# Transposing the attention's softmax weights: one 16-bit transposing transfer in place of four TensorE transposes

## The chip, the cores and the metric

The kernel runs on one core of one Trainium2 chip. A core has five engines, each with its own instruction queue that is worked through in order: TensorE (PE, matrix products; its weight loads are listed as PEld), VectorE (DVE), ScalarE (ACT), GpSimd (POOL) and SyncE (SP), which here only issues transfers. Sixteen DMA engines move the data. Operands lie in SBUF (128 partitions); TensorE writes to PSUM, which is used here as eight banks of 128 x 512 float32. The engines wait for each other through semaphores.

The metric is the time of one execution on the device in microseconds (us), the median of several runs. The profile is of one further execution.

## What is computed

One decoder block on 256 positions of width 2048, all in float32: a normalisation, one wide input projection, two branches (attention and a gated linear recurrence), gates, an output projection, and a gated feed-forward network (FFN). The change touches only the attention:

```python
ATTN_GROUPS = ((128, 1), (512, 4), (2048, 16))      # (window, dilation)
...
for g, (window, dilation) in enumerate(ATTN_GROUPS):
    o_g, lse_g = dilated_window_attention(qh[g], kh[g], vh[g], window, dilation)
    outs.append(o_g)
    lses.append(lse_g)
mix_w = jax.nn.softmax(jnp.stack(lses, axis=0), axis=0)
attn = jnp.einsum('gbhs,gbhsd->bshd', mix_w, jnp.stack(outs, axis=0))
```

There are eight heads with three groups each. A query sees the keys of its group at the group's stride, each group has its own softmax, and the three outputs are mixed by their softmax denominators. This is the same as one softmax over the keys of all three groups together (a key of two groups counted twice), and that is how the kernel computes it.

## The kernel before

**The stream of weights.** Nearly all of the time is matrix products of the activations with weights that are read once. Each float32 product is made of three faster ones: weights and activations are split into a high half (a rounded copy, made by ScalarE) and a low half (the difference, made by VectorE). The main loop runs over "items". In the stage of interest, an item is a chunk of 128 x 1024 weights. For item i the loop emits, in this order: `prepare(i)`, which splits the chunk of item i + 2 (line 365 on ScalarE, line 366 on VectorE, `AHEAD = 2`) and has SP issue loads (`load_pair`, line 270; a pair of chunks fills one of three buffers called raw); `multiply(i)` (line 139, all products); one step of the oldest waiting evacuation of a finished block (lines 240 and 242 add up two banks of accumulation, 888 to 893 apply the rotary tables, 1151 makes gates); `advance_lanes()`, one step of each of two lanes of side work; and `ahead_of_time()`, one step of sums of FFN weights made in advance (`weight_sums`: loads by SP at line 302, sums by VectorE at lines 310 to 314, a store by ScalarE's queue at 317). All instructions stay in this order on each engine (`manual_schedule`), so what is emitted earlier stands ahead in each engine's queue. A split weight chunk has one of three buffers (w), so the split for item i + 2 has to wait until the products of item i - 1 are done.

**The lanes.** They are Python generators: what stands between two `yield`s is emitted in one step, once per item. The recurrence runs in lane 0, twice (half 0, half 1). The attention is taken by lane 1, and by lane 0 too when that is free. It works through a queue of (half, head), four heads for each half of the heads.

**One pass of the attention** is one head and one parity: the 128 queries of even or of odd position. Its 512 scores per query are four blocks of 128 keys: two for the first group (keys of both parities), one for each of the others (keys of the query's parity). A pass takes six steps:

1. TensorE makes the scores in a PSUM bank.
2. VectorE adds the mask and finds the smallest score, whose sign is turned (line 928, into p), and ScalarE takes the exponential with its sum (line 932).
3. VectorE takes the reciprocal of the sum (line 937) and scales p by it (line 938).
4. TensorE transposes the four 128 x 128 blocks of p into a PSUM bank (line 944, against the identity matrix).
5. ScalarE copies the bank to pt in SBUF (line 947), 128 x 512 float32. One more step with nothing follows.
6. TensorE multiplies V with pt, four products that add up to the head's output (in the profile, aux<-pt,v). In the same step the next pass's scores follow.

When a head's two parities are done, `attended` copies its output into the high and low halves for the next projection (lines 966 and 969). p and pt are float32 tiles of 128 x 512 from one ring of five buffers (`ptile`, which also serves the evacuations' short-lived tiles). PSUM banks for the side work (`aux()`) come from a ring of four.

In the first half's passes the items are chunks of the key and query projections; lane 1 works one pass after another beside the recurrence of lane 0, and later both lanes do attention, three steps apart. In the second half's passes (items of the gates and of the recurrence's projection, 12 products of 512 columns each) both lanes are at the same step, so that passes go in pairs.

**Transposing transfers elsewhere.** The FFN turns its activations with `turn_act` (line 1366 on): ScalarE writes the 16-bit halves of each float32 word into two planes (line 1370), SP issues transposing transfers of 128 x 512 two-byte elements (line 1376), and ScalarE joins the transposed planes to words again (line 1385). Its instructions are in the profile of before.

Of the kernel before, what the change touches and what calls it, by code (L numbers as in the profile page):

```python
# [17 lines left out]
U16 = mybir.dt.uint16  # L18
AF = mybir.ActivationFunctionType
OP = mybir.AluOpType  # L20

P = 128
# [79 lines left out]
def tile_hybrid_block(ctx: ExitStack, tc: tile.TileContext, t, out):  # L102
    nc = tc.nc
# [12 lines left out]
    def nm(s):  # L116
        serial[0] += 1
        return f"{s}_{serial[0]}"
# [7 lines left out]
    def aux():  # L126
        return auxp.tile([P, 512], F32, tag="aux", name=nm("aux"))
# [7 lines left out]
    def small(s, n=8, bufs=6):  # L135
        return cpool.tile([P, n], F32, tag=f"small{n}", bufs=bufs, name=nm(s))

    def mm(ps, lhsT, rhs, start, stop):
        nc.tensor.matmul(ps, lhsT, rhs, start=start, stop=stop, skip_group_check=True)  # L139
# [27 lines left out]
    ident = cpool.tile([P, P], F32, name="ident")  # L167
# [38 lines left out]
    def ptile(s):  # L206
        pool, n = (wide_pool[-1], 2) if wide_pool else (fp[0], 5)
        return pool.tile([P, 512], F32, tag="p", bufs=n, name=nm(s))
# [341 lines left out]
            yield  # L550


    class Split:


# [110 lines left out]
    def advance_lanes():  # L666
        tick[0] += 1
        for lane in lanes:
            if not lane and queue:
                lane.append(attention())  # L670
            advance(lane)
# [233 lines left out]
    def attention():  # L905
        done = []
        for _ in range(3):
            if not lanes[0] or tick[0] == beat[0]:
                break
            yield  # L910
        while queue:
            half, h = queue.popleft()
            o = None
            for par in range(2):
                own = slice(par * P, (par + 1) * P)
                ps = aux()
                for g in range(3):
                    q, k = qkT["q", half, g], qkT["k", half, g]
                    if g == 0:
                        mm(ps[:, :S], q[:, h, own], k[:, h, :], True, True)  # L920
                    else:
                        mm(ps[:, P * (g + 1) : P * (g + 2)], q[:, h, own], k[:, h, own], True, True)
                yield
                for part in done[:1]:
                    part()
                p = ptile("p")
                m = small("m")
                nc.vector.tensor_tensor_reduce(
                    out=p, in0=ps, in1=amask[:, par, :], scale=1.0, scalar=3e38,
                    op0=OP.add, op1=OP.min, accum_out=m[:, 0:1],  # L930
                )
                nc.scalar.activation(p, p, AF.Exp, scale=-1.0, bias=m[:, 0:1], accum_out=m[:, 1:2])
                for part in done[1:]:
                    part()
                done = []
                yield
                nc.vector.reciprocal(m[:, 2:3], m[:, 1:2])
                nc.vector.tensor_scalar(p, p, m[:, 2:3], None, op0=OP.mult)
                for _ in range(1):
                    yield  # L940
                ps = aux()
                for c in range(4):
                    cols = slice(c * P, (c + 1) * P)
                    nc.tensor.transpose(ps[:, cols], p[:, cols], ident)  # L944
                yield
                pt = ptile("pt")
                nc.scalar.activation(pt, ps, AF.Copy)
                for _ in range(2):
                    yield
                if o is None:  # L950
                    o = aux()
                for c in range(4):
                    v = vN[half, max(c - 1, 0)][:, c if c < 2 else par, h * P : (h + 1) * P]
                    mm(o[:, own], v, pt[:, c * P : (c + 1) * P], c == 0, c == 3)
            done = attended(4 * half + h, o)
        yield
        for part in done:
            part()
        yield

    def attended(k, o):
        hi, lo, _ = attnT[0](k)
        ov = o[:, :S].rearrange("p (two j) -> p two j", two=2)

        def high():
            nc.scalar.activation(hi.rearrange("p (j two) -> p two j", two=2), ov, AF.Copy)

        def low():
            nc.vector.tensor_sub(
                lo.rearrange("p (j two) -> p two j", two=2), ov,  # L970
                attnT[0].f32(k).rearrange("p (j two) -> p two j", two=2),
            )

        return [high, low]
# [602 lines left out]
    for half in range(2):  # L1577
        for g in range(3):
            c = 1024 * g + 512 * half
# [54 lines left out]
    for i in range(len(items)):  # L1634
        kind, n, _ = items[i]
        b, c = kind[n][:2]
# [99 lines left out]
```

## Time and profile before

| | |
|---|---|
| median of 3 runs | 1688.17 us |
| lowest and highest run | 1687.39 and 1688.42 us |
| the profiled execution | 1689.89 us |
| its span, first to last instruction | 1688.1 us |
| granted TensorE clock, mean | 0.999 of full speed |
| the attention's transposes (line 944) | 64, between 613.9 and 842.1 us |

A row of an instruction group reads: line, engine, operation, output<-inputs by the program's names, shapes, count, then its duration (mean, or smallest/median/largest in ns) and what ended the engine's idle time before it. A row of the timeline begins with the start and the length in us. A row of the chain of waits has the start, the length and the engine that the end of the program can be traced back to. SPq, ACTq and so on are an engine's instruction sequencer: it waits, or issues transfers, while the engine itself does nothing.

### The profile page before, as it was taken

To read this page: it belongs to the slowest core of one execution; us is meant where nothing else is said; L and a number is where in the kernel's file an instruction comes from. 1 tells how busy PE (TensorE), PEld (TensorE's weight loads), DVE (VectorE), ACT (ScalarE), POOL (GpSimd) and SP (SyncE) were. 2 spreads that over 40 slices of the span, in tenths; PEclk is the share of its full clock that TensorE was granted. 3 is DMA by queue.
4 is the path that set the end of the run, shared out by engine and by line. 5 is a ranking of instruction groups with operands and counts; after the bars stand their busy time and mean duration, and the time that the engine had idled before them with its cause. 6 is when DMAs were issued, how large, how long until landed. Compare 5 with 4: busy or idle time off the path is not lost.

```text
span 1688.1 us, 21672 instructions
## 1 busy us (share of the span) xinstructions
PE 1674.2 (99%) x8169; PEld 1406.0 (83%) x8169; DVE 1416.6 (84%) x1623; ACT 983.1 (58%) x1102; POOL 3.9 (0%) x13
## 2 busy tenths in 40 slices
PE   9999999999999999999999999999999999999997
PEld 7888888888888888888888888888888888888886
DVE  6899888867987987776668888898888988898987
ACT  6655555544455545555535547676667666675653
POOL 0000000000000000000000000000000000000000
PEclk9999999999999999999999999999999999999999
DMA  8566666668777866787858556898888888887673
GB/s 278 207 232 242 224 226 227 234 231 298 233 251 250 281 226 225 254 307 264 309 175 274 194 183 209 272 282 270 272 266 283 271 274 266 277 280 267 236 256 128
DMA packets 252841, 419.26 MB, mean 248 GB/s; under 512 B 36752, under 2 KB 103488, under 8 KB 250176
## 3 DMA queue, kind: packets, MB, share of 16 engines
q1 hardware_dynamic: 242480, 379.70, 68.1%
q10 hardware_dynamic: 10192, 38.15, 5.9%
q8 instruction: 64, 1.05, 0.3%
q14 instruction: 41, 0.34, 0.1%
q0 software_dynamic: 64, 0.02, 0.0%
HBM read 376.92 MB, written 35.13 MB: 244 GB/s over the span
## 4 chain that ended last, share of the span: by engine, by line
PE 95%; DVE 2%; ACT 1%; DMA 1%; issue 1%; SPq 0%; DVEq 0%; ACTq 0%
PE acc L139 62%; PE aux L139 32%; DVE wl L421 1%; PE aux L944 0%; DMA raw<-in_w_ffn_gate_up 0%; ACT w L419 0%; DMA x<-in_x 0%; PE aux L611 0%; DVE fz L1509 0%; DVE dl L431 0%; ACT junk L1463 0%; PE aux L598 0%; DVE e L1459 0%; DVE wl L428 0%; DVE f L543 0%
## 5 line engine op out<-in xcount | busy, mean ns | idle before, releaser
L139 PE MATMUL acc<-xT,w 128*128 128x256 f32 (+1 forms) x2048 | 365.1, 338 | 0.0
L421 DVE TENSOR_TENSOR wl<-raw,w 128x2048 fp32r<-128x2048 f32 (+1 forms) x140 | 304.5, 2182 | 67.3 <-ACT w L419 65.3
L139 PEld LDWEIGHTS acc<-xT,w 128*128 128x128 f32 x2048 | 311.9, 188 | 44.7
L366 DVE TENSOR_TENSOR w<-raw,w 128x1024 fp32r<-128x1024 f32 x176 | 215.0, 1222 | 118.9 <-ACT w L365 118.3
L419 ACT ACTIVATE w<-raw 128x2048 fp32r<-128x2048 f32 (+1 forms) x140 | 254.5, 1826 | 97.4 <-PE acc L139 31.6
L365 ACT ACTIVATE w<-raw 128x1024 fp32r<-128x1024 f32 x176 | 185.9, 1058 | 192.8 <-PE acc L139 137.4
L139 PE MATMUL acc<-w,xT 128*128 128x512 f32 x578 | 168.8, 391 | 0.0
L440 ACT ACTIVATE w<-sum 128x1024 fp32r<-128x1024 f32 x57 | 60.6, 1062 | 168.5 <-DVE sum L435 161.7
L139 PE MATMUL acc<-w,hT 128*128 128x512 f32 x472 | 152.7, 391 | 0.4 <-DVE hT L1259 0.4
L448 DVE TENSOR_TENSOR wl<-sum,w 128x1024 fp32r<-128x1024 f32 x114 | 137.2, 1221 | 7.7 <-ACT w L440 7.6
L139 PEld LDWEIGHTS acc<-w,xT 128*128 128x128 f32 x578 | 108.2, 188 | 22.3
L139 PE MATMUL aux<-w,hT 128*128 128x512 f32 x374 | 120.0, 389 | 0.0
L139 PE MATMUL aux<-w,xT 128*128 128x512 f32 x344 | 109.8, 389 | 0.0
L450 DVE TENSOR_TENSOR dl<-raw,dh 128x1536 fp32r<-128x1536 f32 x57 | 100.1, 1757 | 11.3 <-ACT dh L446 8.2
L139 PEld LDWEIGHTS acc<-w,hT 128*128 128x128 f32 x472 | 88.5, 188 | 19.0 <-DVE hT L1259 0.9
L139 PE MATMUL acc<-wl,hT 128*128 128x512 f32 x236 | 91.8, 389 | 0.0
L446 ACT ACTIVATE dh<-raw 128x1536 fp32r<-128x1536 f32 x57 | 84.1, 1475 | 5.3 <-PE acc L139 3.1
L139 PE MATMUL acc<-w,a 128*128 128x512 f32 x268 | 83.7, 389 | 0.2 <-DVE e L1413 0.2
L139 PEld LDWEIGHTS aux<-w,hT 128*128 128x128 f32 x374 | 70.2, 188 | 14.5
L139 PE MATMUL acc<-w,so 128*128 128x512 f32 x240 | 80.4, 389 | 0.0
L139 PE MATMUL aux<-w,a 128*128 128x512 f32 x254 | 79.5, 389 | 0.0
L139 PEld LDWEIGHTS aux<-w,xT 128*128 128x128 f32 x344 | 64.6, 188 | 13.4
(295 smaller groups left out, 2990.2 us busy)
## 6 DMA issues: line engine op xcount, KB each, us to landing
raw<-in_w_in SPq DMA_DIRECT2D x270, 512.0 KB, 4.7
raw<-in_w_ffn_gate_up SPq DMA_DIRECT2D x156, 512.0 KB, 5.0
raw<-in_w_ffn_down SPq DMA_DIRECT2D x88, 512.0 KB, 5.4
pre<-in_w_ffn_gate_up SPq DMA_DIRECT2D x40, 512.0 KB, 6.5
presum<-pre ACTq DMA_DIRECT2D x20, 1024.0 KB, 4.7
s<-presum SPq DMA_DIRECT2D x40, 512.0 KB, 6.9
raw<-in_w_mix_out SPq DMA_DIRECT2D x32, 512.0 KB, 5.0
act<-acts SPq DMA_DIRECT2D x22, 512.0 KB, 6.2
```

What stands on the lines that cost most here:

```text
L139: nc.tensor.matmul(ps, lhsT, rhs, start=start, stop=stop, skip_group_check=True)
L365: nc.scalar.activation(wh, raw, AF.Copy)
L366: nc.vector.tensor_sub(wl, raw, wh.bitcast(F32))
L419: nc.scalar.activation(hi[:, c], raw[:, c], AF.Copy)
L421: nc.vector.tensor_sub(lo[:, c], raw[:, c], hi[:, c].bitcast(F32))
L440: nc.scalar.activation(hi[:, :1024], s[:, :1024], AF.Copy)
L446: nc.scalar.activation(dhi, d, AF.Copy)
L448: nc.vector.tensor_sub(lo[:, c], s[:, c], hi[:, c].bitcast(F32))
L450: nc.vector.tensor_sub(dlo, d, dhi.bitcast(F32))
```

## The change

The four TensorE transposes of a pass, their PSUM bank and ScalarE's copy out of it go. In their place ScalarE splits the 32-bit words of the normalised p into two planes of 16-bit halves (into the tile pt, used as scratch), one transfer issued by SP transposes all eight 128 x 128 blocks of 16-bit elements back into p, and ScalarE joins the two transposed planes of p to words in pt. The bits are moved unchanged. The copy apart and the transfer are emitted in the step of the normalisation (step 3 above), the join three steps later, one step ahead of the products with V. A pass has as many steps as before.

```diff
+    def halves_apart(flat, words):
+
+        nc.scalar.activation(
+            flat.bitcast(U16).rearrange("p (z c) -> p z c", z=2),
+            words.bitcast(U16).rearrange("p (c z) -> p z c", z=2), AF.Copy,
+        )
+
+    def halves_joined(words, planes):
+
+        nc.scalar.activation(
+            words.bitcast(U16).rearrange("p (c z) -> p z c", z=2), planes, AF.Copy
+        )
+
...
                 nc.vector.reciprocal(m[:, 2:3], m[:, 1:2])
                 nc.vector.tensor_scalar(p, p, m[:, 2:3], None, op0=OP.mult)
-                for _ in range(1):
+                pt = ptile("pt")
+                halves_apart(pt, p)
+                nc.sync.dma_start_transpose(
+                    p.bitcast(U16).rearrange("p (n q) -> p n q", n=8), pt.bitcast(U16)
+                )
+                for _ in range(3):
                     yield
-                ps = aux()
-                for c in range(4):
-                    cols = slice(c * P, (c + 1) * P)
-                    nc.tensor.transpose(ps[:, cols], p[:, cols], ident)
+                halves_joined(pt, p.bitcast(U16).rearrange("p (z c) -> p z c", z=2))
                 yield
-                pt = ptile("pt")
-                nc.scalar.activation(pt, ps, AF.Copy)
-                for _ in range(2):
-                    yield
                 if o is None:
                     o = aux()
```

## The prediction

> **What bounds the kernel now.** I read the page first, for which engine is full; then the chain of waits, cut to the stage in which the attention runs; then the rows of the removed instructions.
>
> ```profile
> PE 1674.2 (99%) x8169; PEld 1406.0 (83%) x8169; DVE 1416.6 (84%) x1623; ACT 983.1 (58%) x1102; POOL 3.9 (0%) x13
> PE 95%; DVE 2%; ACT 1%; DMA 1%; issue 1%; SPq 0%; DVEq 0%; ACTq 0%
> by line: PE acc L139 82.4%; PE aux L139 14.4%; PE aux L944 2.9%; PE aux L1137 0.4%; issue 0.1%
> L944 PE MATMUL aux<-ident,p x64: 270/273/328, 614.0 to 842.1; 128*128 128x128 f32 x64
> 600.00:740.00 140.00, 139.85 (x889) 124.54 (x888) 109.86 (x177) 76.90 (x132) 0.00 (x0) 1.00 0.72 246
> 740.00:852.00 112.00, 112.00 (x575) 95.32 (x574) 74.23 (x107) 59.24 (x78) 0.00 (x0) 1.00 0.80 282
> 852.00:1688.00 836.00, 825.60 (x3668) 681.39 (x3666) 730.29 (x760) 518.32 (x506) 0.00 (x0) 1.00 0.76 248
> ```
>
> The first line says that TensorE is busy for 99% of the span; the second that it makes up 95% of the chain that ended last. The third is the chain's share by line for 600 to 850 us alone: nothing but TensorE, with the removed transposes (L944) at 2.9%. The last three give, for each stretch: length, PE, PEld, DVE, ACT, POOL, clock, DMA share, GB/s. PE stands still for 0.15 us in the attention's 252 us, at full clock, with DMA at 0.72 and 0.80. So an instruction removed from PE here is worth its whole place in PE's row, as long as nothing new makes PE wait.
>
> **What the change removes.** 64 transposes (16 passes: 8 heads, 2 parities, 4 each). The mean duration of 273 ns is no price, since matmuls overlap. Their place in the chain is 2.9% of 250 us = 7.2 us; from the pieces of the chain:
>
> ```profile
> 614.14 0.44 PE aux L944 x4
> 779.03 0.87 PE aux L944 x8
> ```
>
> 0.44 us for one pass, 0.87 for two passes side by side, so 16 x 0.44 = **7.0 us**. I take 7.0. Also removed: ScalarE's copy of the transposed bank, 0.59 us per pass, and one PSUM bank per pass. Nothing on PE waits for a bank in this stage (its idle time above), so I give the bank nothing.
>
> **What it adds on ScalarE.** The same pair of copies and the same kind of transfer already run in the FFN:
>
> ```profile
> L1370 ACT ACTIVATE e<-e x20: 1037/1042/1060, 1089.7 to 1468.8; 128x1024 uint16<-128x1024 uint16 x20
> L1385 ACT ACTIVATE act<-e x20: 1337/1374/1385, 1101.5 to 1482.2; 128x1024 uint16<-128x1024 uint16 x20
> L947 ACT ACTIVATE pt<-aux x16: 576/588/612, 614.6 to 843.1; 128x512 f32<-128x512 f32 x16
> ```
>
> Planes apart cost 1.04 us, joined 1.37, less the old 0.59: 1.82 us more per pass, 29 us in all, on an engine with 136 of 252 us busy. That is hidden if the weight splits queued behind it (L365, then VectorE's L366) still beat PE. The worse part is a new wait: the copy apart stands in ScalarE's queue ahead of the next split, and it waits for VectorE's normalisation L938. The tightest place I found is the first pair of passes in the second half:
>
> ```profile
> 776.39 1.06 ACT L365 ACTIVATE w<-raw 128x1024 fp32r<-128x1024 f32 x1 [1.66 <-PE acc L139]
> 777.47 1.28 ACT L1151 ACT_TABLE_LOAD   x1
> 778.76 0.69 ACT L1151 ACTIVATE gate<-acc,r1c 128x512 f32<-128x512 f32 x1
> 776.09 0.49 DVE L938 TENSOR_SCALAR p<-p,m 128x512 f32<-128x512 f32 x1
> 776.69 0.49 DVE L938 TENSOR_SCALAR p<-p,m 128x512 f32<-128x512 f32 x1
> 777.48 1.23 DVE L366 TENSOR_TENSOR w<-raw,w 128x1024 fp32r<-128x1024 f32 x1 [0.31 <-ACT w L365]
> 779.66 8.45 PE L139 MATMUL acc<-w,xT 128*128 128x512 f32 x36
> 787.95 1.05 PE L139 MATMUL aux<-pt,v 128*128 128x128 f32 x8
> ```
>
> Both normalisations end at 777.2. ScalarE then does: apart 776.6 to 777.7, apart 777.7 to 778.7, the split of 776.39 only now, 778.7 to 779.8; VectorE's low half follows, to 781.1. PE's 36 matmuls are three weight chunks of 2.82 us; this split feeds the second, which began at 779.66 + 2.82 = 782.5 and begins 0.87 earlier without the transposes, at 781.6. Half a microsecond is left. The next: table load, gate, split to 782.8, low half to 784.1, wanted at 784.4: 0.3 us. So ScalarE fits, barely. Of the eight single passes of the first half, the tightest I found is the fourth:
>
> ```profile
> 676.13 0.49 DVE L938 TENSOR_SCALAR p<-p,m 128x512 f32<-128x512 f32 x1
> 677.86 1.22 DVE L366 TENSOR_TENSOR w<-raw,w 128x1024 fp32r<-128x1024 f32 x1
> 681.04 5.82 PE L139 MATMUL acc<-xT,w 128*128 128x512 f32 x32
> 686.70 1.05 PE L139 MATMUL aux<-pt,v 128*128 128x128 f32 x8
> ```
>
> Apart 676.6 to 677.7, split to 678.8, its low half 678.8 to 680.0 in place of 677.86 to 679.1, wanted by the chunk at 681.04, now 680.6: 0.6 us left. I allow a stall of 0.25 us for each of the four pairs, **1.0 us** in all; the bounds are 0 and, if every one of 12 steps (8 single, 4 pairs) lost 0.5 us, 6.0. In the same bounds goes that pt is claimed two steps earlier from a ring of five buffers: with two passes under way, seven are claimed in six steps, one comes round after 4.3, and pt is held for 4. That fits, so I cost it at nothing.
>
> **What it adds on SP and DMA.** One transfer per pass of 128x1024 two-byte elements, on SP's queue, behind the weight loads (L270) and ahead of the loads for the weight sums (L302). Its kind:
>
> ```profile
> L1376 SPq DMA_TRANSPOSE e<-e x40: 1217/1610/2399, 1093.5 to 1476.8; - x40
> DMA to landing us min/median/max: 2.5/6.0/8.3
> SPq L270 <- DVE w L366: 138.0, 29, 8.1
> SPq L270 <- DVE m L937: 56.2, 9, 8.5
> 776.01 0.88 SPq L270 DMA_DIRECT2D raw<-in_w_in  x2
> 781.68 7.66 SPq L270 DMA_DIRECT2D raw<-in_w_hgrn_branch  x4
> raw<-in_w_in SPq DMA_DIRECT2D x270, 512.0 KB, 4.7
> ```
>
> Those 40 are 128x512, half the size, so I double the issue: 3.2 us on SP (bounds 1.2, were it fixed, and 4.8). From issue to landing they took 2.5 to 8.3 us, in a stage where four are issued in a row behind loads; twice the data is given 1.6 us of issue and 0.5 of moving more: 4.6 at best, 8.1 in the middle, 10.4 at worst.
>
> The time allowed: from the end of a normalisation to the first product with V is 787.95 - 776.6 = 11.4 us in the pair; the shortest is the fourth pass, 676.6 to 686.7, 10.1 us. Less 1.04, 1.37 and the 0.44 saved, 7.2 us are left for the transfer. SP mostly sleeps in its wait for a free weight buffer (L270); if that wait stands ahead of the transfer, up to 8 us are lost. But the waits ended by L937 show where the transfer falls: the load is released by the split just before the reciprocal (776.01 against L938 at 776.09), and the next load is issued 5.7 us later, at 781.68. The transfer is issued into that hole, and its packets run behind one pair of weight loads only. I take 5.5 us, nearer the best case than the FFN's middle, because here nothing else is queued ahead: inside 7.2. In a pair the second transfer is issued some 3 us after the first, and its product is 1.8 us later, against a window of 11.4, not 10.1: it also fits, with about 1 us.
>
> What is queued behind: the L302 loads come 2 to 6 us later. They feed L310 on VectorE, which can then be held up by 1 to 2 us in the few passes in which both fall together; this is in the 1.0 us above. The weight loads come up to 3 us later, but a buffer is filled six chunks (17 us) before its use and lands in 4.7.
>
> The Trainium skill ("Advanced Engine Details and Errata", X-Bar Transpose) calls such transposes as fast as plain DMAs; by it the transfer's share of the DMA engines is about 1 us per pass, an estimate, and no term changes.
>
> **The sum.** 7.0 removed, 1.0 given back: 6.0 us. The profiled execution took 1689.9 us with a span of 1688.1, and goes to 1683.9 and 1682.1; the median of the runs is 1688.2, so I predict **1682.2**. The measurement cannot tell less than about 0.2% (3.4 us) from no change: faster begins at 1684.8.
>
> **Rivals.**
> - Late splits. The copies apart and the joins hold up ScalarE and VectorE more than I allow, 0.3 to 0.5 us of room being overrun in all 12 steps: 6.0 us given back, 1687.2; with only the pairs overrun by 1 us each, 1685.2. For it: the sums above, and L938 ends where VectorE is 78% busy. Against: the work saved on ScalarE by the old copy.
> - Late transfer, **the slower side**. The join waits for the landing, PE for the join. It decides from 7.2 us on; each step that is late by x costs x. With the FFN's middle, 8.1, 12 steps lose 0.9: 10.8 less 7.0, 3.8 slower, 1692.0. For it: that median, and the issue time that was never seen for this size. Against: the hole in SP's queue, and the FFN's transfers standing four in a row.
> - Blocks one after another. If the whole issue-to-landing time doubles with the size, 12.0 us at the median, each step loses 4.8: 57.6 less 7.0, 1738.8. The Trainium skill ("VectorE: DVE Perf Modes", The three transpose paths) speaks that way: 1309 ns by DMA for one 128x128 block against 390 on TensorE, whose use it advises; eight in a row would be over 10 us. The best landing above speaks against it: four blocks in 2.5 us.
> - Saved but given back. After 852 us PE is idle for 10.4 us in 836; if a later stage runs at DMA's or VectorE's pace, the 7 us turn into idle time there: 1688. PE's 99% there speaks against.
>
> **How the numbers follow.** Forecast (1680.5 to 1684.7) 0.67; late splits 0.15; given back 0.04; late transfer 0.11; blocks in a row 0.03. So faster 0.67, same 0.19, slower 0.14. The range runs from all 7.0 saved, with half a microsecond of scatter, 1680.5, to the end of the cases without loss, 1688.0; outside are the slower cases and a little below.
>
> **What would show it.** Right: L944 is gone; in 600 to 850 us the chain is still all TensorE, PE's idle time stays near 1 us, and the attention's last product comes some 6 us earlier. The new transposes land within 7 us of their issue, and the join's line shows little idle time released by DMA. Wrong: PE waits for pt or for w in that stretch (late transfer, late splits), or the stretch is shorter and PE's idle time after 852 us grows by as much (given back). I would be most wrong if the issue on SP took far longer than 3 us.

## The result, and the profile after

The changed kernel takes **1706.97 us**, the median of 4 runs (1703.08 to 1708.23), beside 1687.88 us for the kernel before (4 runs, 1687.39 to 1688.42): a ratio of 1.0107, with a 95% interval of 1.0095 to 1.0120. It is 1.1% slower, where 6 us less had been forecast. The profiled execution took 1707.22 us, with a span of 1705.4 us and a mean granted clock of 0.992.

In kernel.py of after the two copies of ScalarE stand at lines 555 (planes apart) and 562 (planes joined), the transfer at 954; the lines of the attention that were there before stand 13 lower (the smallest score 941, exponential 945, reciprocal 950, normalisation 951, rotary tables 901 to 906). The lines up to 552, so 139, 242, 270, 302, 310 to 317, 365 and 366, have not moved.

First the page of after (busy time by engine, and the chain of waits), then the chain between 600 and 850 us by line.

```profile
PE 1677.9 (98%) x8105; PEld 1407.4 (83%) x8105; DVE 1416.2 (83%) x1623; ACT 1007.2 (59%) x1118; POOL 3.8 (0%) x13
PE 92%; DVE 3%; ACT 2%; DMA 2%; issue 1%; ACTq 0%; DVEq 0%
```

```profile
by line: PE acc L139 46.2%; PE aux L139 11.9%; DMA p<-pt 11.4%; DVE w L366 7.1%; issue 6.0%; ACT w L365 4.4%; ACT pt L562 2.2%; DVE w L905 1.2%; DVE sum L904 1.2%; DVE p L941 1.2%; DVE sum L242 1.1%; DVE p L951 1.0%; ACT w L901 0.8%; DVE qk
```

PE has 64 instructions fewer, as meant, and is busy for longer (1677.9 us, before 1674.2). Between 600 and 850 us the chain was all TensorE before; now TensorE is 58.1% of it, the transfer p<-pt 11.4%, the copy that joins (L562) 2.2%, and the splits and the work ahead of them (L365, L366, L904, L905, L941, L951) most of the rest.

Where in the span? I cut both traces at the same places of the program: the first half's stretch runs from the first product of the 84th of the 128 chunks of the key and query projections to the last product of the 128th, the second half's on to the first product of the attention's own projection, and that projection up to the output projection. The windows of before, then of after (length, then busy time of PE, PEld, DVE, ACT, POOL, granted clock, DMA share, GB/s):

```profile
598.63:752.73 154.10, 153.95 (x970) 136.86 (x969) 122.00 (x193) 84.01 (x141) 0.00 (x0) 1.00 0.73 251
752.73:857.71 104.98, 104.98 (x529) 88.98 (x529) 66.33 (x95) 54.67 (x72) 0.00 (x0) 1.00 0.78 270
```

```profile
597.21:767.99 170.78, 158.42 (x938) 139.67 (x937) 122.31 (x193) 96.02 (x149) 0.00 (x0) 0.95 0.79 239
767.99:875.92 107.93, 104.14 (x497) 87.02 (x496) 65.51 (x95) 66.76 (x80) 0.00 (x0) 0.98 0.91 282
875.92:922.20 46.28, 46.28 (x218) 38.29 (x216) 35.67 (x47) 22.17 (x23) 0.00 (x0) 1.00 0.57 185
```

Length less PE's busy time is PE's idle time: in the first half 0.15 us before and 12.36 after, in the second 0 and 3.79. The second loss is the clock: a mean of 0.95 of full speed over 170.78 us is 8.5 us lost (from the clock's own records: 8.53, and 1.71 in the second half; 1.3 of the 8.5 fall on time in which PE stands anyway). Take that off, and PE's work at full clock fell from 153.95 to 151.2 us and from 104.98 to 102.4: 2.8 and 2.5, so **5.3 us of the 7.0 did go**. Against that stand 16.0 us of new idle time and 8.9 of half clock: 19.6 us more in the two stretches. The rest of the span is 2.3 us shorter; 1.4 of that lies before 597 us, where the change has no part.

What PE waited for, by the view of the waits, in after between 600 and 870 us (in all, times, the longest; before, this list is empty):

```profile
PE aux L139 <- ACT pt L562: 13.9, 5, 4.2
PE acc L139 <- DVE w L366: 1.5, 2, 0.8
PE acc L139 <- ACT w L365: 0.7, 1, 0.7
```

So 13.9 us are five waits of the products with V for the joined pt, and only 2.2 us are waits for split weights. What such a wait does to the clock is seen in three neighbouring windows around the longest of the five:

```profile
685.00:689.90 4.90, 0.69 (x4) 0.32 (x3) 1.29 (x2) 1.39 (x2) 0.00 (x0) 0.87 1.02 300
689.90:695.30 5.40, 5.40 (x20) 4.93 (x21) 3.98 (x7) 3.41 (x7) 0.00 (x0) 0.50 1.05 362
695.30:712.00 16.70, 16.70 (x98) 14.53 (x96) 10.88 (x17) 7.73 (x12) 0.00 (x0) 1.00 0.64 145
```

PE stands for 4.2 us, then works at a granted clock of 0.50 for 5.4 us. By the clock records the four waits of 4.21, 3.14, 3.60 and 2.34 us were followed by half clock for 6.8, 3.4, 6.8 and 3.4 us, and the fifth, of 0.65 us, by none. The Trainium skill ("TensorE: Matmul & The Clock Gate", Why this matters for your kernels) asks for no idle gaps of TensorE over about 3 us, since one window of idle halves the clock; this trace agrees, except that 2.34 us were enough.

**Four ways in which pt came late.** The first is seen in the chain of waits of after that ends in the longest stall:

```profile
677.36 11.06 DMA p<-pt
...
688.51 1.35 ACT pt L562
...
689.90 2.50 PE aux L139 x9
```

The transfer is issued as soon as the planes are apart, but lands only 11.06 us later. In that time ScalarE's queue has the store of the FFN's weight sums (L317). The view of the DMA from 677 to 689 us, before and then after (packets, MB, share of the engines' time; below, the median us to landing):

```profile
q10 hardware_dynamic: 144, 1.05, 20.7%
presum<-pre ACTq DMA_DIRECT2D x1, 1024.0 KB, 5.7
```

```profile
DMA  5999999999999000000066946025999949969999
q10 hardware_dynamic: 144, 1.05, 53.1%
presum<-pre ACTq DMA_DIRECT2D x1, 1024.0 KB, 10.3
p<-pt SPq DMA_TRANSPOSE x1, 11.1
```

The store's same 1.05 MB took 20.7% of the engines' time beside plain loads and 53.1% beside the transfer, and landed after 10.3 us and not 5.7; in between, the engines stood nearly still (the zeros, some 2 us).

The second way has nothing to do with the landing. The timeline of after (start, length):

```profile
701.41 1.23 SPq L954 DMA_TRANSPOSE p<-pt  x1
712.43 0.49 DVE L951 TENSOR_SCALAR p<-p,m 128x512 f32<-128x512 f32 x1
712.95 1.06 ACT L555 ACTIVATE pt<-p 128x1024 uint16<-128x1024 uint16 x1 [2.01 <-DVE p L951]
713.91 1.32 ACT L562 ACTIVATE pt<-p 128x1024 uint16<-128x1024 uint16 x1
715.29 1.56 PE L139 MATMUL aux<-pt,v 128*128 128x128 f32 x8 [3.14 <-ACT pt L562]
```

This transfer landed at 707.78, but its join begins at 713.91. The two lanes are three steps apart, so this lane's join is emitted in the very step in which the other lane's planes are taken apart, behind it in ScalarE's queue; and that copy waits for VectorE's normalisation, which ends at 712.92. The next but one pass did the same: joined 7.58 us after its landing, with a stall of 3.60.

The third way is SP's queue:

```profile
708.01 10.33 SPq L270 DMA_DIRECT2D raw<-in_w_in  x4
718.43 1.26 SPq L954 DMA_TRANSPOSE p<-pt  x1
```

The transfer of the planes that were taken apart from 712.95 to 714.00 is issued at 718.43: SP slept in a wait of L270 for a free weight buffer. This befell the sixth and the eighth of the eight passes of the first half (4.4 us each).

The fourth way is loads issued just ahead, among them those of the weight sums (L302). It befell the first pass and the second pair of the second half, whose two transfers are merged in the second row:

```profile
813.00 0.93 SPq L302 DMA_DIRECT2D pre<-in_w_ffn_gate_up  x2
813.99 8.03 SPq L954 DMA_TRANSPOSE p<-pt  x2
```

The first transfer of that pair landed 9.2 us after its issue began, that of the first pass 9.3 us, with no store under way.

What each way cost is seen from the five waits for pt: 4.21 us in the fourth pass (the landing beside the store), 3.14 and 3.60 in the fifth and the seventh (the join's place in ScalarE's queue), 2.34 in the second pair of the second half and 0.65 in the first pass (the loads ahead). The third way cost nothing here: in the sixth and the eighth pass no product waited. It comes to bear in the experiments.

The transfer itself, by its line (smallest, median and largest duration of the issue in ns; then us to landing):

```profile
L954 SPq DMA_TRANSPOSE p<-pt x16: 1232/1882/4047, 612.3 to 862.3; - x16
DMA to landing us min/median/max: 5.0/6.3/11.1
```

Counted from the end of the copy apart, the eight passes of the first half landed after 9.7, 5.4, 8.1, 11.1, 6.4, 9.7, 5.0 and 10.0 us.

### The profile page after: what moved, and what is told of

Its sections match the earlier page's. It is cut to its first block, busy times and chain, and to the rows that moved or that the text cites. A ratio compares the mean times of both kernels' runs of the same rounds, so it can differ in the third digit from the quotient of the medians.

```text
span 1705.4 us, 21609 instructions
## 1 busy us (share of the span) xinstructions
PE 1677.9 (98%) x8105; PEld 1407.4 (83%) x8105; DVE 1416.2 (83%) x1623; ACT 1007.2 (59%) x1118; POOL 3.8 (0%) x13
## 4 chain that ended last, share of the span: by engine, by line
PE 92%; DVE 3%; ACT 2%; DMA 2%; issue 1%; ACTq 0%; DVEq 0%
PE acc L139 58%; PE aux L139 33%; DMA p<-pt 2%; DVE w L366 1%; ACT w L365 1%; DVE wl L421 0%; PE aux L624 0%; ACT pt L562 0%; DVE fz L1520 0%; ACT w L419 0%; ACT junk L1474 0%; DVE w L905 0%; DVE sum L904 0%; DVE p L941 0%; DVE sum L242 0%
## 5 line engine op out<-in xcount | busy, mean ns | idle before, releaser
L366 DVE TENSOR_TENSOR w<-raw,w 128x1024 fp32r<-128x1024 f32 x176 | 214.6, 1222 | 136.5 <-ACT w L365 136.3
L365 ACT ACTIVATE w<-raw 128x1024 fp32r<-128x1024 f32 x176 | 184.4, 1054 | 145.9 <-PE acc L139 96.2
```

What stands on the lines that cost most here:

```text
L365: nc.scalar.activation(wh, raw, AF.Copy)
L366: nc.vector.tensor_sub(wl, raw, wh.bitcast(F32))
```

## The experiments

Two theories stood against each other. **The landing**: the transfer is late, by SP's queue and by other transfers. **The order on ScalarE**: two more copies per pass, each behind something that waits, make pt late whatever the transfer does. That half clock follows and doubles the bill belongs to both. The table has all runs; the stretches are cut as above, "idle" is length less PE's busy time, "clock" the us lost to half clock by the clock's records. The ratios are against the kernel before, run on the same chip. The stretches are those of one profiled execution each, and the executions of one kernel lie apart by several us (after: 1703.08 to 1708.23, e_joins: 1699.43 to 1708.00), so a difference of 2 or 3 us between two changed kernels says little. By the ratios, the intervals of e_second, e_copies and e_copies_joins lie clear below that of after, and that of e_both3 above it; the others touch it or overlap with it, and what is read from them rests on their rows.

| kernel | median us | ratio (95%) | first half us | idle | clock | second half us | idle | clock |
|---|---|---|---|---|---|---|---|---|
| before | 1687.88 | | 154.10 | 0.15 | 0 | 104.98 | 0 | 0 |
| after | 1706.97 | 1.0107 (1.0095 to 1.0120) | 170.78 | 12.36 | 8.53 | 107.93 | 3.79 | 1.71 |
| e_first | 1703.15 | 1.0084 (1.0069 to 1.0099) | 169.30 | 11.72 | 6.83 | 104.84 | 0 | 0 |
| e_second | 1687.89 | 0.9996 (0.9987 to 1.0006) | 154.11 | 0.15 | 0 | 104.62 | 1.73 | 0 |
| e_joins | 1702.74 | 1.0090 (1.0066 to 1.0113) | 164.69 | 9.88 | 1.71 | 107.70 | 4.50 | 0 |
| e_held | 1706.56 | 1.0110 (1.0095 to 1.0125) | 162.46 | 9.01 | 1.71 | 105.69 | 2.51 | 1.71 |
| e_copies | 1697.97 | 1.0061 (1.0043 to 1.0079) | 163.89 | 5.14 | 5.12 | 105.22 | 0.03 | 0 |
| e_copies_joins | 1692.87 | 1.0026 (1.0015 to 1.0036) | 159.58 | 3.58 | 1.71 | 105.31 | 0 | 0 |
| e_steps | 1701.24 | 1.0081 (1.0065 to 1.0097) | 157.25 | 6.21 | 0 | 106.05 | 0 | 0 |
| e_filler | 1702.41 | 1.0083 (1.0067 to 1.0099) | 165.39 | 3.48 | 0 | 105.25 | 2.74 | 0 |
| e_both | 1705.07 | 1.0097 (1.0082 to 1.0112) | 161.57 | 8.94 | 0 | 105.61 | 3.54 | 0 |
| e_both3 | 1727.92 | 1.0242 (1.0223 to 1.0260) | 163.16 | 8.09 | 1.71 | 108.31 | 4.83 | 0 |
| e_pool | 1702.50 | 1.0094 (1.0068 to 1.0120) | 174.68 | 15.58 | 8.53 | 106.90 | 3.50 | 1.71 |
| e_pool_held | 1707.45 | 1.0111 (1.0094 to 1.0128) | 166.64 | 9.64 | 6.83 | 104.03 | 2.24 | 0 |
| e_joinpool | 1704.84 | 1.0101 (1.0086 to 1.0116) | 168.11 | 12.01 | 3.41 | 107.43 | 4.31 | 0 |

### Where: one half of the heads at a time

```diff
+                if half == 0:      # e_first; in e_second: half == 1
                     pt = ptile("pt")
                     halves_apart(pt, p)
...
+                else:
+                    yield
+                    ps = aux()
...
+                    nc.scalar.activation(pt, ps, AF.Copy)
```

> Transfer in the eight single passes of the first half of the heads only; TensorE transposes kept in the second half. Theory (few stalls of TensorE, each followed by a stretch of half clock, make the loss; both are read from the changed kernel's trace): the first half there has 12.4 us of idle time and 17 us at half clock (8.5 us lost) against 3.5 us saved, so some 17 us slower than before, about 1705. Rival (every pass pays about the same, since each transfer is late): half of the whole loss, about 1697. Rival (the later stages pay): 1688 or less.

> Transfer in the four pairs of passes of the second half only; TensorE transposes kept in the first. Theory: the second half has 3.8 us of idle time and 1.7 us lost to the half clock against 3.5 us saved: 2 us slower than before, about 1690. Rival (every pass pays the same): about 1697.

The windows of the two stretches in e_second:

```profile
598.04:752.15 154.11, 153.96 (x970) 136.86 (x969) 122.04 (x193) 84.09 (x141) 0.00 (x0) 1.00 0.72 251
752.15:856.77 104.62, 102.89 (x497) 85.44 (x496) 65.64 (x95) 66.58 (x80) 0.00 (x0) 1.00 0.93 291
```

With the change in the first half alone the ratio is 1.0084; with it in the second alone there is no difference that can be told (0.9987 to 1.0006). The second half shows what was hoped for, and why it does not pay: PE works for 102.89 us and not 104.98, 2.1 less, and 1.73 of that come back as idle time, by the waits 1.4 us for late splits (L365, L366) and 0.3 for pt. The loss is made in the first half, so the other experiments are read there. (In after the second half too is 3.0 us longer than before, with a stall of 2.34 us that e_second does not have: that part comes only with the change in the first half, and why was not tried.)

### The order on ScalarE: joins ahead of the lanes

In e_joins a pass's join is emitted at the start of its step, ahead of what the other lane emits in it; nothing else moves.

```diff
+        while joins and joins[0][0] <= tick[0]:
+            joins.popleft()[1]()          # in advance_lanes, ahead of the lanes
...
-                for _ in range(3):
+                joins.append((tick[0] + 3, lambda ...: halves_joined(...)))
+                for _ in range(4):
                     yield
-                halves_joined(pt, p.bitcast(U16).rearrange("p (z c) -> p z c", z=2))
-                yield
```

> The changed kernel with one order changed: a join due in a step is emitted ahead of both lanes' work of that step, so that it no longer stands behind the other lane's copy apart in ScalarE's queue. Theory: the stalls at 712 and 737 us (3.1 and 3.6 us, with 5.1 us lost to the half clock behind them), where the transfer had landed 6 and 8 us before its join began, go: about 1695. Rival (those stalls come from the late transfer or from VectorE): no change, 1707.

The waits of PE from 600 to 890 us in e_joins:

```profile
PE aux L139 <- ACT pt L562: 9.3, 8, 2.3
PE acc L139 <- DVE w L366: 3.4, 6, 0.8
PE acc L139 <- ACT w L365: 1.6, 2, 0.9
```

The first half took 164.69 us, 6.1 less than after, with 2.5 us less idle time and 1.71 us of half clock in place of 8.53. The order was part of it, and far from all: the stage is still 10.6 us longer than before. Five waits for pt became eight shorter ones. The stalls of the fifth and the seventh pass fell to 0.53 and 0.36 us; but now the sixth and the eighth, whose transfers SP issued 3.3 us late, stalled for 1.58 and 2.25 us, with joins that began within 0.12 us of their landing. So the third way had been hidden behind the second. The waits for split weights grew from 2.2 to 5.0 us; two of them, at 736 and 737 us, are for splits behind a copy apart that had waited 2.63 us for its normalisation. PE's work at full clock is 1.9 us higher than in after, which no row here explains.

### The landing: the store held back

In e_held the store of the weight sums waits while a transposed pass is between its two copies.

```diff
+    in_flight = [0]
...
+            while in_flight[0]:
+                yield
             pre[n] = dram.tile(...)
...
                 halves_apart(pt, p)
+                in_flight[0] += 1
...
                 halves_joined(pt, ...)
+                in_flight[0] -= 1
```

> The changed kernel, in which the store of the FFN weight sums (1 MB to DRAM, on ScalarE's queue) is put off while a transposing transfer is between its issue and its join. Theory: where both overlapped, at 677 to 688 us, packets of the store took 3.4 us in place of 0.3 and the transfer landed 11 us after it was ready; that stall of 4.2 us and 3.4 us of lost clock go: about 1699. Rival (the transfer is as slow without the store, for the loads ahead of it): no change, 1707.

The view of the DMA from 677 to 689 us in e_held, then its windows (first half, second half, projection; all lines below 294 stand a few lower), then its waits of PE from 600 to 890:

```profile
presum<-pre ACTq DMA_DIRECT2D x1, 1024.0 KB, 4.5
p<-pt SPq DMA_TRANSPOSE x1, 7.1
```

```profile
597.69:760.15 162.46, 153.45 (x938) 134.94 (x937) 116.45 (x185) 95.86 (x149) 0.00 (x0) 0.99 0.77 231
760.15:865.84 105.69, 103.18 (x497) 86.80 (x496) 68.80 (x100) 66.95 (x80) 0.00 (x0) 0.98 0.94 293
865.84:920.68 54.84, 49.73 (x217) 40.22 (x216) 38.25 (x51) 21.96 (x23) 0.00 (x0) 0.94 0.62 205
```

```profile
PE aux L139 <- ACT pt L565: 10.7, 5, 4.4
PE acc L139 <- ACT w L368: 4.6, 1, 4.6
```

One after the other, the same store lands after 4.5 us and the same transfer after 7.1, of which the issue took 3.57. That the two hold each other up is shown; by what in the DMA engines is not. The stall of the fourth pass is gone, and the first half is 8.3 us shorter than in after, the second 2.2. The fifth pass now stalls for 4.42 us: the sums' loads have moved to just ahead of its transfer, which landed 8.9 us after its issue began. Then the attention's projection, 46.28 us in after, takes 54.84: the held sums are finished there, and PE stands 4.6 us for a split (L368), which stands in ScalarE's queue behind the store; the store waits for the sums, and these for their loads (6.00 us). The gain went to later waits, and the whole time stayed where it was.

### The copies without the transfer

In e_copies TensorE transposes as before; the two copies are made at the places that they have in after, but what they write is overwritten by the copy of the bank. So no transposing transfer runs, and the only new load is on ScalarE. The bank's copy (0.60 us, which the change does not have) stands behind the join, one step later than in before. In e_copies_joins the join and the bank's copy stand ahead of the lanes, as in e_joins.

```diff
                 halves_apart(pt, p)
-                nc.sync.dma_start_transpose(...)
-                for _ in range(3):
+                yield
+                ps = aux()
+                for c in range(4):
+                    cols = slice(c * P, (c + 1) * P)
+                    nc.tensor.transpose(ps[:, cols], p[:, cols], ident)
+                for _ in range(2):
                     yield
                 halves_joined(pt, ...)
+                nc.scalar.activation(pt, ps, AF.Copy)
```

> ScalarE's work of the change without its transfer: the copy apart and the join run in their new places (the join's output is overwritten), but TensorE transposes p as before and a third copy takes its bank to pt right behind the join. Theory (the landing of the transfer is what is late): 1688 to 1691. Rival (the copies in ScalarE's queue, with their wait for VectorE, make the loss by themselves): 1700 or more, with the stalls of the fifth and seventh pass still there.

> ScalarE's copies without the transfer, as in the run that cost 10 us, with one order changed: join and bank copy are emitted ahead of both lanes' work of their step, so that they do not stand behind the other lane's copy apart and its wait for VectorE. Theory (that place in the queue is the whole cost of the copies): no stall of over 1 us, 1688 to 1690. Rival (the copies delay the weight splits, or the copy apart waits anyway): 1694 or more.

The timeline of e_copies at its largest stalls, and the waits of PE in e_copies_joins:

```profile
705.48 0.49 DVE L951 TENSOR_SCALAR p<-p,m 128x512 f32<-128x512 f32 x1
706.00 1.06 ACT L555 ACTIVATE pt<-p 128x1024 uint16<-128x1024 uint16 x1 [2.01 <-DVE p L951]
706.96 1.32 ACT L562 ACTIVATE pt<-p 128x1024 uint16<-128x1024 uint16 x1
708.32 0.60 ACT L962 ACTIVATE pt<-aux 128x512 f32<-128x512 f32 x1
708.97 2.08 PE L139 MATMUL aux<-pt,v 128*128 128x128 f32 x8 [2.23 <-ACT pt L962]
```

```profile
PE aux L961 <- DVE p L954: 2.5, 2, 1.9
PE aux L139 <- ACT pt L964: 1.1, 1, 1.1
```

**With no transfer at all the kernel is 0.6% slower than before** (1.0043 to 1.0079), and the first half is 9.8 us longer: 5.0 of new idle time, and nearly all the rest half clock. The rows show it: ScalarE waits 2.01 us for the normalisation before it may take the planes apart, and the other lane's join and pt stand behind that. With the joins ahead, 4.3 of the 9.8 us go. What stays, 5.5 us, I put down to the weight of the copies: TensorE's transposes now wait for a normalisation (2.5 us in the rows above) that comes later, as VectorE's chain (split, smallest score, exponential, normalisation) runs through a ScalarE with 2.4 us more per pass; that reading fits the rows and was not tried by itself.

### A longer window

e_steps is e_first with the join two steps later. For that, p and pt need six buffers and not five; two small tables were moved or cut to make room.

```diff
-                    for _ in range(3):
+                    for _ in range(5):
                         yield
                     halves_joined(pt, ...)
...
-        pool, n = (wide_pool[-1], 2) if wide_pool else (fp[0], 5)
+        pool, n = (wide_pool[-1], 2) if wide_pool else (fp[0], 6)
```

> Transfer in the first half only, as in the run that has it in the first half alone (1703), but with the join and the products with V two steps later (5.6 us more), and one more buffer in the ring of p and pt (room from two small tables that move or shrink). Theory (the result is only late): the stalls go and the saved 3.5 us show: about 1685. Rival (load on ScalarE, VectorE or DMA slows the weight splits): 1695 or more.

The first half took 157.25 us with no half clock, 12.1 less than in e_first: two steps more took most of the loss away, and 3.1 us over before were left. But the whole kernel gained only 1.9 us, as the part ahead of the attention took 604.55 us and not 597.00. The groups of the commonest products between 10 and 350 us, in before and in e_steps (count, busy time, mean ns):

```profile
L139 PE MATMUL acc<-w,xT 128*128 128x512 f32 x384 | 123.2, 391 | 0.0
```

```profile
L139 PE MATMUL acc<-w,xT 128*128 128x512 f32 x381 | 124.0, 395 | 0.0
```

The same products took 395 ns and not 391, with no idle time. What differs there is where the tiles lie in SBUF; that this is the cause was not tried by itself.

### The price of a stall

e_filler fills three of the gaps: 16 idle products (`keep_warm`, in the kernel already) stand ahead of the products with V of the fourth, fifth and seventh pass.

```diff
+                passes[0] += 1
+                if passes[0] in (4, 5, 7):
+                    keep_warm(16)
```

> The changed kernel with 16 idle products (3.4 us, bfloat16, on zeros, into a spare bank) on TensorE ahead of the products with V in the fourth, fifth and seventh pass, where TensorE stood still for 4.2, 3.1 and 3.6 us. Theory (standing still is what halves the clock): the stretches at half clock after 688, 715 and 739 us go, 8.5 us: about 1698. Rival (the clock falls for another reason, or the idle time is all that counts): 1707 or more.

The window of e_filler's first half:

```profile
597.89:763.28 165.39, 161.91 (x986) 138.36 (x985) 121.57 (x193) 96.19 (x149) 0.00 (x0) 1.00 0.80 243
```

pt comes no earlier by it, and the work added is useless, but the clock is 1.00 in both halves and the first half is 5.4 us shorter than after (ratio 1.0083 for 1.0107). So the half clock followed from the idle time and was a price of its own.

### Both together, and on GpSimd

e_both is e_joins and e_held in one; e_both3 has one step less between the loads of the weight sums and their use, meant to get the sums done before the projection.

```diff
-            for _ in range(4):      # e_both3, in weight_sums
+            for _ in range(3):
```

> The changed kernel with joins emitted first and the store of the weight sums put off, the loads awaited four steps as before. Awaiting them three steps only had cost 16 us of idle time ahead of the attention. Theory (both causes add up): in the first half of the attention the 10 us that putting off the store brought there and the 5 to 6 of the joins together leave it 1 to 4 us longer than before; the second half 1 us longer; and 8.5 us are lost in the attention's projection, where two late jobs are forced through: 1699 to 1702. Rival (both act on the same stalls): 1706.

> The changed kernel with joins emitted first, the store of the weight sums put off while a transfer is under way, and the sums' loads awaited for three steps in place of four, so that the sums are done before the attention's projection (putting the store off alone left two jobs for 870 to 887 us, where TensorE stood still for 5.1 us and lost 3.4 to the clock). Theory (order in ScalarE's queue and the store make the stalls): about 1690. Rival (transfers are late without either): 1697 or more.

e_both's first half is 161.57 us at full clock, hardly less than with either edit alone (164.69, 162.46): the two do not add. It still stands idle for 8.94 us, and 6.7 of these are three waits for pt (1.57, 2.99 and 2.10 us in the first, fifth and eighth pass) whose join began within 0.1 us of its landing: the first two transfers were issued right behind four loads, the third 3.3 us late by SP's sleep. With the order and the store mended, the landing is what is left. The projection gives 8.3 us back (54.56), as in e_held. e_both3 was a miss: the projection is back at 46.28 us, but ahead of the attention VectorE waits for the loads of the sums (L311, 11.1 us) and PE with it, and that part takes 621.64 us.

GpSimd is nearly idle, so it was given both copies (e_pool; with e_held's edit e_pool_held) or the join alone (e_joinpool).

```diff
-        nc.scalar.activation(
+        nc.gpsimd.tensor_copy(      # halves_joined; in e_pool halves_apart too
             words.bitcast(U16).rearrange("p (c z) -> p z c", z=2), planes
         )
```

> The changed kernel with the copy apart and the join on GpSimd, which does nothing else in this stage, so that neither stands in ScalarE's queue. What is known: ScalarE's copies without the transfer cost 10 us. Theory (half of the loss is the order in ScalarE's queue, the rest the transfer's landing): the stalls of the fifth and seventh pass go, those of the fourth pass and of the second pair stay: about 1697, if a copy takes GpSimd no more than 2 us. Rival (its copies take much longer, which no trace here shows): the joins come later in every pass, 1710 or more.

> GpSimd's copies and the store put off, together. Theory: the attention's two halves take no longer than before, or less (down to 7 us less), and 8.5 us are lost in its projection: 1690 to 1697. Rival (GpSimd too slow): as the run with GpSimd alone.

> The changed kernel with only the join on GpSimd (1.6 us there), the copy apart on ScalarE. With both on GpSimd the join stood behind the other lane's copy apart there just as on ScalarE; here nothing but another join stands ahead of it, and what is left is the landing of the transfer. Theory: the stalls of the fifth and seventh pass, whose transfers landed 6 and 8 us before their join, go with the clock lost behind them; those of the fourth pass and the second pair, where the transfer landed last, stay, 0.3 us longer: 1694 to 1698. Rival (the landing is late in those passes too): 1703 or more.

The group of the joins of e_joinpool in 600 to 870 us:

```profile
L562 POOL COPY pt<-p 128x1024 uint16<-128x1024 uint16 x16 | 26.7, 1684 | 489.8 <-ACT w L901 272.6 <-DMA p<-pt 189.2 <-ACT w L365 28.1
```

With both copies on GpSimd the first half of the profiled execution is longer (174.68 us; that execution is the longest of e_pool's runs, which lie between 1700.5 and 1711.2), the waits for pt add up to 19.0 us, and the longest is 6.1: a join stands behind the other lane's copy apart there too. e_pool_held, with 166.64 us for the first half, loses 8.5 us in the projection again. With the join alone there (e_joinpool) it stands behind nothing, and all joins of the first half begin within 0.2 us of their landing; the stage is 2.7 us shorter than after, where e_joins gained 6.1. As in e_joins, the stalls of the fifth and the seventh pass go and the sixth and the eighth stall instead, for 2.08 and 2.94 us. A further reason is in its window of the first half:

```profile
597.23:765.34 168.11, 156.10 (x938) 136.34 (x937) 128.48 (x193) 86.67 (x141) 12.98 (x8) 0.98 0.82 243
```

VectorE's same 193 instructions take 128.48 us, in after 122.31. Its work got slower where it ran beside GpSimd's copies: of the splits (L366) between 590 and 880 us, the ten that did took 1.63 us in the mean and up to 2.33, the other 73 at most 1.23. So a free engine was no free place for the copy.

**What follows.** Neither theory does alone. In e_copies the copies cost 9.8 us in the first half without any transfer; the collision with the store is worth 8.3 us there with the order as it was; each is partly hidden behind the other, and half clock enlarges both. With both mended, late landings remain. Left open: what in the DMA engines makes a transfer behind four loads, or beside a store, land so late; what makes up the 5.5 us of e_copies_joins; and why the half clock follows some pauses and not others. No version tried beats the kernel before.

## Why the prediction was wrong

**What the change removes** was right in kind and taken too large: line 944's transposes are gone, and PE's work at full clock fell by 5.3 us where 7.0 were forecast. In stretches of other runs that have no half clock it fell by between 1.3 us (e_both, first half: 161.57 less 8.94 idle, for 153.95) and 3.2 (e_pool_held, second half) where 3.5 were due. Why less goes than the transposes' place in the chain stays open.

**What it adds on ScalarE** was right in the copies' durations (1.06 and 1.35 us, for 1.04 and 1.37) and in the splits' order of size: PE waits 2.2 us for late splits, and 1.0 was allowed. The step failed in what it looked at. "ScalarE fits, barely" followed the split behind the copy apart, in a pair of the second half and in one pass of the first that had no other pass beside it. It did not follow the join behind the other lane's copy apart, when both lanes do attention three steps apart: joins came 6.1 and 7.6 us after their landings there, with stalls of 3.14 and 3.60 us. e_copies, with one copy of 0.60 us per pass more than the change has, gives 9.8 us for the copies by themselves; 4.3 of these go when the joins are put ahead.

**What it adds on SP and DMA** is the other step that failed. The issue was taken too dear: 1.23 us at the least and 1.88 in the middle, not 3.2; it does not double with the size. "The transfer is issued into that hole, and its packets run behind one pair of weight loads only" was wrong in five of eight passes. I read the hole off passes where the wait for a weight buffer had just ended; the sixth and the eighth pass found SP asleep in it. The third and the fourth met the weight sums' store, and the first had four loads issued ahead of it, two of them the L302 loads that the prediction put 2 to 6 us behind. So 5.5 us became 5.0 to 11.1, against a window of 7.2. Of these five only the fourth cost much (4.21 us and the clock behind it) and the first a little (0.65): the window of 7.2 was the shortest, and the others had more. The bounds, 4.6 to 10.4, nearly held; the value taken within them did not, and the store, which runs on ScalarE's queue, was not in the list of what is queued ahead at all.

**The rivals.** "Late transfer", given 0.11 and 1692.0 us, is the nearest to what happened, and about half of it: its sign (PE waits for the join, the join for the landing) holds for 7.2 of the 13.9 us of waits for pt. The other 6.7 us are joins that stood behind the other lane's copy apart, with the transfer long landed, and no rival had that. Its price was too low as well, since "each step that is late by x costs x" leaves out the clock: 16.0 us of new idle time cost 8.9 more. "Late splits" is 2.2 us of after's waits, and 1.4 of the 1.73 us of idle time by which the second half of e_second gives back the 2.1 us of work that it saves. "Given back" meant a stage after 852 us, and that did not happen: from the output projection on, PE's idle time was 10.5 us before and 10.2 after. "Blocks one after another" can be dropped: the Trainium skill ("VectorE: DVE Perf Modes", The three transpose paths) gives 1309 ns for a block by DMA, which for eight would be 10.5 us, an estimate; here eight landed 5.0 us after the issue began at best, and 6.3 in the middle. The advice of the Trainium skill to use TensorE (the same page, Rules for kernel authors) held all the same.

**The sum.** 7.0 gained and 1.0 lost was forecast; 5.3 gained, 16.0 lost to idle time and 8.9 to the clock came out, less 2.3 us by which the rest of this execution's span was shorter. The range ended at 1688.0, since a transfer that was in time in the passes looked at was taken to be in time in all.

## What to carry to other kernels

Before work is moved off a full engine, list every pass of the loop, not the tightest two: where the second lane stands, what the issuing queue sleeps in, and which loads and stores run at that moment; the worst pass sets the window. Ask of each new instruction what stands ahead of it in its engine's queue and what that waits for. Price a stall of TensorE of over 2 us at more than its length, as the clock often fell after such a one here.

## What the runs showed of the hardware

- After a pause of TensorE, or from its last part on, the granted clock was often 0.50 for 3.4 us or twice that. In the profiles of after and the thirteen experiments this followed all 15 pauses of over 3.1 us, and 11 of the 20 between 2.0 and 3.0 us.
- A 1 MB store and a transposing transfer of 128 x 1024 two-byte elements, under way at once, landed after 10.3 and 11.1 us; one after the other, after 4.5 and 7.1.
- The issue of that transfer took 1.23 us at the least, as long as that of half the size (1.22 in the FFN's row).
- GpSimd's copy that joins two planes of 128 x 512 two-byte elements took 1.68 us in the mean, ScalarE's 1.35; eight of them in a stretch went with 6.2 us more of VectorE's busy time, and VectorE's splits under way beside such a copy took 1.63 us in the mean and not 1.22.
- Products of 128 x 128 by 512 columns took 395 ns and not 391 in one kernel (e_steps), in which some tables had other places in SBUF; that this is the cause was not tested.
